# Operands straight from the turned banks, their sums and differences on GpSimd, and the last square from its bank, in a hybrid SSD and attention layer

## The chip, the cores and the metric

The kernel runs on one core of a Trainium2 chip. A core has five engines that work through queues of their own and wait for one another by semaphores: TensorE (PE; its weight loads are listed as PEld), VectorE (DVE), ScalarE (ACT), GpSimd (POOL) and SyncE (SP), which issues most DMAs. Matrix products go to banks of PSUM; VectorE and ScalarE read banks and SBUF tiles, and in this kernel GpSimd reads and writes SBUF tiles only. The metric is the device time of one execution in microseconds, as a median of several runs.

## The reference

One decoder layer of 1024 tokens and 1024 channels, all in float32:

```python
h = _rmsnorm(x, pre_g)
proj = jnp.einsum('bld,de->ble', h, w_in)        # z, xBC, dt, q, k, v, f, gates: 9248 columns
...                                              # branch A: convolution and chunked SSD scan; branch B: attention
merged = jax.nn.sigmoid(g_ssm) * p_ssm + jax.nn.sigmoid(g_att) * p_att
out = jnp.einsum('bld,de->ble', merged, w_out)
return x + _rmsnorm(out, post_g)
```

The change touches the beginning (the norm of x and the operands of the first product) and the very end (the norm of the last 128 rows of the result).

## The kernel before

**Products.** The three large products (w_in, the two branch weights, w_out) are made two output blocks at a time by a seven-product scheme instead of eight products: class `Pair` works on two blocks of 128 output columns (or rows), and its steps 1 to 7 multiply sums of weight blocks with sums of blocks of the other operand. A product keeps float32 accuracy by splitting each operand in a high part (rounded to `fp32r`) and a low part (the rest), and by three matmuls: high by high, low by high, high by low (`matmuls`, with `mm` at line 130). Weights are split by `Pair.split` (lines 351 and 352: ScalarE rounds, VectorE subtracts), sums of weights are made by `total` (line 357). `keep` (line 404) and `give` (lines 412 to 418) take a finished bank out.

**Operands.** For the first product the other operand is the normed x, turned so that channels lie on partitions. With x in four blocks of 512 by 512 (`b11` and `b21` from the first 512 tokens, `b12` and `b22` from the second) the operands are b11, b21, t1 = b12 - b11, -t2 with t2 = b22 - t1, t3 = t2 - b11, t4 = t2 - b21 and -b22. Each has a high tile and a low tile in SBUF with four blocks of 128x512: in the profile x0 is b11, x1 is b21, x2 is -b22, x3 is t1, x4 is -t2, x5 is t3 and x6 is t4, with h or l behind it.

**Prologue** (lines 1132 to 1241). `norm_tiles` squares each 128x1024 tile of x (line 1160 on VectorE for two tiles, line 1162 on ScalarE for the others), makes the reciprocal root (1163, 1164) and scales the tile (1166 on VectorE for the first four tiles, 1168 on GpSimd for the second four). `turned` turns one block of 128 channels of four tiles into a bank `pt` of 128x512 (line 1173; `turn` is line 133), of which there are two. For the first half of the tokens, each of the eight banks is copied into the float32 tile `low`, times pre_norm_g (line 1192 on ScalarE, line 1194 on VectorE for the first two). `put` then makes the high part from `low` (line 1178, ScalarE) and the low part (line 1180, VectorE). For the second half, in four rounds, two banks are copied to `up` and `b22` (line 1212, ScalarE); four float32 matmuls with `wdf` into `df` read `low` and these copies; then come t1 (1218), t2 (1221) and their parts, and the differences t3 and t4, which are written over `low` (1225, 1226, VectorE). Their parts and those of -b22 follow.

**Order.** `Stream` lists all steps of all pairs in one order written out by hand; `halves(n)` issues the next n half steps of six matmuls each. TensorE's queue keeps the order of the program. The queues of the other engines are ordered when the program is built, by the order of the program, by `high_priority` blocks, and by the times that a planner gives to each instruction; `pin` keeps an instruction in the order of the program. On the chip each queue is worked through in that order. In the prologue the stream runs four half steps between the banks 4 to 7 of the first half, one in each of the four rounds, and six after them (the products `pb`, `pd`, `pc`).

**End.** The last four pairs multiply with w_out. For each block of 128 tokens, `outcome` receives two banks of 512 columns as `o[ch]`; `post` squares each (line 1101, ScalarE, with the row's sum in `ssq`), multiplies it by post_norm_g (line 1104) and, after the second one, adds the two sums (1108, VectorE), takes root and reciprocal (1109, 1110), and scales, adds x and stores (1112, 1113). The very last bank is step 4 of the last pair: `give` copies it with its sign turned (line 412, ScalarE) before `post` works on the copy.

Of the kernel before, what the change touches and what calls it, by code (L numbers as in the profile page):

```python
# [16 lines left out]
P = 128  # L17
T = 1024
D = 1024
# [67 lines left out]
def hybrid_layer(ctx: ExitStack, tc, a, out):  # L87
# [50 lines left out]
    def small(name="th"):  # L138
        return gp.tile([P, HALF], F32, tag="th", name=name)
# [182 lines left out]
    class Pair:  # L322
# [7 lines left out]
        def __init__(self, keys, handlers, ops=None, adds=nc.vector):  # L330
            self.keys, self.handlers = keys, handlers
            self.ops = xop if ops is None else ops
            self.adds = adds
            self.raw, self.op, self.prepared = {}, {}, set()
            self.s1, self.sums = None, 0

        def load(self, names):
            for n in names:
# [82 lines left out]
        def do(self, which):  # L421
            if which in (2, 4, 3) or which in (5, 7) and self.sums:
                unit, ch = {2: (0, 0), 4: (1, 0), 3: (0, 1)}.get(which, (1, 1))
                for begin in self.handlers[unit][2:]:
                    begin(ch)
            if which == 1:
                pool, tag = self.bank
                self.b = pool.tile([P, HALF], F32, tag=tag, bufs=1, name="pb")
                yield from self.matmuls(self.b, 1, "b11", True)
                self.k1 = self.keep(self.b)  # L430
            elif which == 2:
                pool, tag = self.other
                ps = pool.tile([P, HALF], F32, tag=tag, bufs=1, name="p" + tag)
                yield from self.matmuls(ps, 2, "b21", True)
                self.give(0, 0, ps, self.k1, "sum")
            elif which == 6:
                yield from self.matmuls(self.b, 6, "-t2", False)
                self.k2 = self.keep(self.b)
            elif which in (5, 7):
                if which == 5:  # L440
                    self.c = pj.tile([P, HALF], F32, tag="c", bufs=1, name="pc")
                    yield from self.matmuls(self.c, 5, "t1", True)
                else:
                    yield from self.matmuls(self.b, 7, "t3", False)
                    self.k7 = self.keep(self.b)
                self.sums += 1
                if self.sums == 2:
                    self.give(1, 1, self.c, self.k7, "less")
            elif which == 4:
                yield from self.matmuls(self.b, 4, "t4", False)  # L450
                self.give(1, 0, self.b)
            elif which == 3:
                yield from self.matmuls(self.c, 3, "-b22", False)
                self.give(0, 1, self.c, self.k2, "from")
# [609 lines left out]
    def merge(i):  # L1064
# [17 lines left out]

        return dst, post, begin

    def outcome(i):

        o, g, xr, st = {}, {}, {}, {}

        def begin(ch):
            xr[ch] = wp.tile([P, KH, P], F32, tag="raw", bufs=6, name="xr").rearrange("p a b -> p (a b)")  # L1090
            nc.sync.dma_start(xr[ch], a["x"][i * P : (i + 1) * P, half(ch)])

        def dst(ch):
            o[ch] = fin["pool"].tile([P, HALF], F32, tag="ot", bufs=5, name="ot")
            return o[ch]

        def post(ch):
# [3 lines left out]
            nc.scalar.activation(small("sq").bitcast(BF16)[:, 0:HALF], o[ch], AF.Square, accum_out=ssq[:, ch : ch + 1])  # L1101

            g[ch] = small("g") if i >= 6 else o[ch]
            (nc.vector if i >= 6 else nc.gpsimd).tensor_tensor(g[ch], o[ch], fin["postg"][:, half(ch)], ALU.mult)
            if len(o) < 2:
                return
            r = ssq[:, 0:1]
            nc.vector.tensor_tensor(r, r, ssq[:, 1:2], ALU.add)
            nc.scalar.activation(r, r, AF.Sqrt, bias=eps4, scale=1.0 / D)
            nc.vector.reciprocal(r, r)  # L1110
            for c in range(2):
                nc.vector.scalar_tensor_tensor(o[c], g[c], r, xr[c], ALU.mult, ALU.add)
                (nc.sync, nc.scalar)[c].dma_start(out[i * P : (i + 1) * P, half(c)], o[c])

        return dst, post, begin

# [7 lines left out]
    def final(kind, i, handler, ops, adds):  # L1124
        return Pair(((kind, 2 * i), (kind, 2 * i + 1)), (handler(2 * i), handler(2 * i + 1)), ops, adds)

    ends = [final("wbs", i, gated, ops_s, nc.vector) for i in range(4)]
    ends += [final("wba", i, merge, ops_a, nc.gpsimd) for i in range(4)]
    ends += [final("merged", i, outcome, ops_w, nc.gpsimd if i > 1 else nc.vector) for i in range(4)]


    with tc.tile_pool(name="pro", bufs=1, reuse_waits="tile", side="right") as pro, tc.tile_pool(
# [23 lines left out]
        def norm_tiles(hf, tiles):  # L1156
            for t, xt in enumerate(tiles, 4 * hf):
                sqt = small("sqt").bitcast(BF16)
                if t in (1, 3):
                    nc.vector.tensor_tensor_reduce(sqt, xt, xt, 1.0, 0.0, ALU.mult, ALU.add, ss[:, t : t + 1])  # L1160
                else:
                    nc.scalar.activation(sqt, xt, AF.Square, accum_out=ss[:, t : t + 1])
                nc.scalar.activation(rstd[:, t : t + 1], ss[:, t : t + 1], AF.Sqrt, bias=epst, scale=1.0 / D)
                nc.vector.reciprocal(rstd[:, t : t + 1], rstd[:, t : t + 1])
                if hf == 0:
                    nc.vector.tensor_scalar(xt, xt, rstd[:, t : t + 1], None, ALU.mult)
                else:
                    nc.gpsimd.tensor_scalar(xt, xt, rstd[:, t : t + 1], None, ALU.mult)

        def turned(tiles, k):  # L1170
            pt = prop.tile([P, HALF], F32, tag="pt", bufs=2, name="pt")
            for j in range(4):
                turn(pt[:, j * P : (j + 1) * P], tiles[j][:, k * P : (k + 1) * P]) 
            return pt
# [13 lines left out]
        stream.begin()  # L1188
        for k in range(NK):
            pt = turned(tiles, k)  # L1190
            if k > 1:
                nc.scalar.activation(low[:, k, :], pt, AF.Copy, scale=preg[:, k : k + 1])
            else:
                nc.vector.tensor_scalar(low[:, k, :], pt, preg[:, k : k + 1], None, ALU.mult)
# [9 lines left out]
        for j in range(KH):  # L1204
# [17 lines left out]
                put("-t2", j, t2, -1.0)  # L1222
            stream.halves(1)

            nc.vector.tensor_tensor(b11, t2, b11, ALU.subtract)
            nc.vector.tensor_tensor(b21, t2, b21, ALU.subtract)
        dft = small("dft")
        nc.scalar.activation(dft, df, AF.Identity, bias=bdf)
        stream.halves(1)
# [470 lines left out]
```

## Time and profile before

| | |
|---|---|
| median of 3 runs | 1325.71 us (1322.34 to 1330.65) |
| profiled execution | 1329.54 us, span 1327.8 us |
| mean granted clock of TensorE | 0.986 |
| busy: TensorE, VectorE, ScalarE, GpSimd | 96%, 77%, 59%, 23% of the span |
| DMA | 233.59 MB, mean 176 GB/s |

The span runs from the first to the last instruction that the profiler recorded. Busy time of TensorE includes waiting inside its pipeline. In rows of the timeline the first number is the start, the second the duration in us, then engine, line, operation, tiles and shapes; in brackets stands the idle time of the engine before it and what ended that. A merged row has "xN" at its end. In rows of groups the numbers after the bar are busy us and mean ns of one. Times are counted from the span's start.

### The profile page before, as it was taken

The page shows a single profiled execution, that of the slowest core. Times are in us where ns is not written, and L with a number is a line of the kernel's source. Part 1 is how long each engine was busy: PE and PEld are TensorE (multiplying, and loading weights), DVE is VectorE, ACT ScalarE, POOL GpSimd, SP SyncE. Part 2 cuts the span into 40 slices and gives each one's busy share as a digit, 9 for nine tenths or more (in the row PEclk, how much of TensorE's full clock was granted, in tenths as well). Part 3 has the DMA queues.
Part 4 walks back from the last instruction along what each step waited for, and adds up shares of the span by engine and source line. Part 5 has one row for each costly group of instructions (what it writes and reads, how often), then busy time and mean ns, then how long its engine had stood idle before and what let it go on. Part 6 is the DMA issues. An engine that isn't in the chain of part 4 may idle for free.

```text
span 1327.8 us, 21035 instructions
## 1 busy us (share of the span) xinstructions
PE 1271.5 (96%) x7054; PEld 995.1 (75%) x7054; DVE 1021.1 (77%) x1977; ACT 789.8 (59%) x1726; POOL 304.2 (23%) x311
## 2 busy tenths in 40 slices
PE   6899999999999999899999999999989998899997
PEld 4578888788878788688777677777766776678886
DVE  6878888798789878787767667666788666886975
ACT  7645665566556756566555565666666555644654
POOL 3000340024102410142001223131111212246152
PEclk9899999999999999899999999999999999999999
DMA  8132543645363546345464557565677556656933
GB/s 289 59 115 67 161 141 120 195 136 150 127 206 128 136 148 186 115 124 184 164 231 159 196 172 236 200 206 180 225 244 240 194 181 230 223 176 200 364 125 103
DMA packets 154668, 233.59 MB, mean 176 GB/s; under 512 B 17216, under 2 KB 62656, under 8 KB 154560
## 3 DMA queue, kind: packets, MB, share of 16 engines
q1 hardware_dynamic: 142016, 205.53, 48.4%
q0 software_dynamic: 6400, 16.10, 3.2%
q10 hardware_dynamic: 6144, 10.62, 2.1%
q8 instruction: 55, 0.90, 0.3%
q14 instruction: 53, 0.43, 0.1%
HBM read 162.99 MB, written 72.34 MB: 177 GB/s over the span
## 4 chain that ended last, share of the span: by engine, by line
PE 64%; DVE 11%; DMA 10%; ACT 8%; issue 5%; SPq 1%; POOL 0%; DVEq 0%; ACTq 0%
PE pb L130 26%; PE pc L130 14%; PE pd L130 5%; PE av L130 4%; PE s L130 4%; PE pt L133 4%; ACT ex L1463 2%; PE yps L130 2%; DMA raw<-in_wu 2%; DVE wop L352 2%; ACT wop L351 1%; DVE sum L357 1%; PE tr L133 1%; PE st L130 1%; DVE ex L1459 1%
## 5 line engine op out<-in xcount | busy, mean ns | idle before, releaser
L1463 ACT ACTIVATE ex<-ex,nm 128x512 f32<-128x512 f32 (+1 forms) x192 | 116.1, 607 | 146.7 <-DVE nm L1459 142.7
L352 DVE TENSOR_TENSOR wop<-sum,wop 128x512 fp32r<-128x512 f32 x178 | 141.4, 795 | 66.0 <-ACT wop L351 65.4
L351 ACT ACTIVATE wop<-sum 128x512 fp32r<-128x512 f32 x178 | 111.4, 626 | 77.7 <-DVE sum L357 25.6
L404 ACT ACTIVATE s<-pb 128x512 f32<-128x512 f32 x144 | 85.2, 592 | 93.7 <-PE pb L130 89.9
L352 DVE TENSOR_TENSOR wop<-raw,wop 128x512 fp32r<-128x512 f32 x146 | 107.0, 734 | 42.7 <-ACT wop L351 41.6
L130 PE MATMUL pc<-x3h,wop 128*128 128x512 f32 x384 | 131.8, 401 | 1.9 <-DVE th L418 0.9
L130 PE MATMUL pb<-x0h,wop 128*128 128x512 f32 x384 | 133.0, 404 | 0.0
L130 PE MATMUL pb<-x6h,wop 128*128 128x512 f32 x384 | 131.2, 399 | 1.2 <-ACT s L404 1.2
L130 PE MATMUL pb<-x4h,wop 128*128 128x512 f32 x384 | 130.2, 396 | 0.7 <-ACT x4h L1178 0.7
L130 PE MATMUL pc<-x2h,wop 128*128 128x512 f32 x384 | 130.4, 398 | 0.3 <-DVE u L756 0.3
L130 PE MATMUL pb<-x5h,wop 128*128 128x512 f32 x384 | 129.1, 395 | 0.7 <-ACT s L404 0.7
L1459 DVE CUSTOM_DVE_ANT_0 ex<-s,fb 128x512 f32<-128x512 f32 (+1 forms) x192 | 95.7, 552 | 33.1 <-PE s L130 33.1
L351 ACT ACTIVATE wop<-raw 128x512 fp32r<-128x512 f32 x146 | 90.7, 623 | 12.7 <-PE pc L130 6.4
L133 PE MATMUL pt<-ident,ex 128*128 128x128 f32 x576 | 80.5, 285 | 11.6 <-ACT ex L1463 10.6
L130 PE MATMUL pd<-x1h,wop 128*128 128x512 f32 x272 | 91.2, 394 | 0.0
L130 PEld LDWEIGHTS pc<-x3h,wop 128*128 128x128 f32 x384 | 73.3, 191 | 20.5 <-ACT wop L351 1.9
L133 PEld LDWEIGHTS pt<-ident,ex 128*128 128x128 f32 x576 | 68.9, 145 | 24.8 <-ACT ex L1463 19.2
L130 PEld LDWEIGHTS pb<-x6h,wop 128*128 128x128 f32 x384 | 73.0, 190 | 18.3 <-ACT s L404 1.6
L130 PEld LDWEIGHTS pb<-x0h,wop 128*128 128x128 f32 x384 | 74.3, 193 | 16.5 <-issue 0.7
L130 PEld LDWEIGHTS pb<-x4h,wop 128*128 128x128 f32 x384 | 72.3, 188 | 17.5 <-ACT x4h L1178 1.2
L213 POOL TENSOR_TENSOR wd<-wd 128x256 f32<-128x256 f32 x32 | 32.7, 1021 | 229.7 <-DMA wd<-in_wo 128.9
L130 PEld LDWEIGHTS pb<-x5h,wop 128*128 128x128 f32 x384 | 72.1, 188 | 17.4 <-ACT s L404 1.1
(310 smaller groups left out, 3021.2 us busy)
## 6 DMA issues: line engine op xcount, KB each, us to landing
raw<-in_wu SPq DMA_DIRECT2D x128, 256.0 KB, 3.5
csb<-cs_dram SPq DMA_DIRECT2D x32, 256.0 KB, 5.1
fb<-f_dram SPq DMA_DIRECT2D x16, 512.0 KB, 6.7
rb<-st_dram SPq DMA_DIRECT2D x48, 128.0 KB, 3.0
wd<-in_wo SPq DMA_DIRECT2D x40, 128.0 KB, 3.3
xt<-in_x SPq DMA_DIRECT2D x8, 512.0 KB, 5.9
gs_dram<-th ACTq DMA_DIRECT2D x16, 256.0 KB, 4.0
qh_dram<-th SPq DMA_DIRECT2D x16, 256.0 KB, 4.8
```

The source lines that it names most:

```text
L130: return tc.keep_in_program_order(nc.tensor.matmul(*args, **kw))
L133: return tc.keep_in_program_order(nc.tensor.transpose(out_, in_, idn))
L213: pin(nc.gpsimd.tensor_tensor(t[out_], t[a_], t[b_], ALU.subtract))
L351: nc.scalar.activation(op[:, 0], src, AF.Copy)
L352: nc.vector.tensor_tensor(op[:, 1], src, op[:, 0], ALU.subtract)
L357: self.adds.tensor_tensor(t, x, y, ALU.add)
L404: nc.scalar.activation(s, ps, AF.Copy)
L1459: nc.vector.tensor_tensor_reduce(o, s[e][:, 0:w], fb[hp, h][:, e, 0:w], 1.0, 3.0e38, ALU.add, ALU.min, nm)
L1463: pin(nc.scalar.activation(o, o, AF.Exp, scale=-1.0, bias=nm, accum_out=hd.at(hd.sm, i, h, e)))
```

## The change

Four edits in the prologue and one at the end:

- The four tiles of the second half are scaled by VectorE too, no longer by GpSimd.
- For the first half, ScalarE makes the high part from the bank itself (times pre_norm_g), VectorE makes the low part from the bank and the high part, and GpSimd then adds the two into `low`. The copy into `low` and the use of `put` on it go. A bank is free only once the low part is made; there are three banks `pt` instead of two.
- The differences t3 and t4 are made by GpSimd instead of VectorE.
- Of the last block of 128 tokens (i = 7), the last bank is no longer copied: ScalarE squares it where it is, VectorE multiplies it by -1 and post_norm_g, and the sum of squares of the other half enters the root as its bias, scaled beforehand.

```diff
@@ class Pair, step 4
-                self.give(1, 0, self.b)
+                (self.closing or (lambda ps: self.give(1, 0, ps)))(self.b)
@@ outcome
+        def finish(r):
+            nc.vector.reciprocal(r, r)
+            for c in range(2):
+                nc.vector.scalar_tensor_tensor(o[c], g[c], r, xr[c], ALU.mult, ALU.add)
+                (nc.sync, nc.scalar)[c].dma_start(out[i * P : (i + 1) * P, half(c)], o[c])
+
+        def closing(ps):
+
+            r, g[0] = st["ssq"][:, 0:1], small("g")
+            with tc.high_priority():
+                nc.scalar.activation(dst(0).bitcast(BF16)[:, 0:HALF], ps, AF.Square, accum_out=r)
+                nc.vector.scalar_tensor_tensor(g[0], ps, -1.0, fin["postg"][:, half(0)], ALU.mult, ALU.mult)
+                nc.scalar.activation(r, r, AF.Sqrt, bias=st["ssq"][:, 1:2], scale=1.0 / D)
+                finish(r)
...
+            if i == 7:
+                nc.vector.tensor_scalar(ssq[:, ch : ch + 1], ssq[:, ch : ch + 1], 1.0 / D, eps4, ALU.mult, ALU.add)
...
+    ends[-1].closing = closings[7]
@@ prologue
-                if hf == 0:
-                    nc.vector.tensor_scalar(xt, xt, rstd[:, t : t + 1], None, ALU.mult)
-                else:
-                    nc.gpsimd.tensor_scalar(xt, xt, rstd[:, t : t + 1], None, ALU.mult)
+                nc.vector.tensor_scalar(xt, xt, rstd[:, t : t + 1], None, ALU.mult)
...
-            pt = prop.tile([P, HALF], F32, tag="pt", bufs=2, name="pt")
+            pt = prop.tile([P, HALF], F32, tag="pt", bufs=3, name="pt")
...
-            if k > 1:
-                nc.scalar.activation(low[:, k, :], pt, AF.Copy, scale=preg[:, k : k + 1])
-            else:
-                nc.vector.tensor_scalar(low[:, k, :], pt, preg[:, k : k + 1], None, ALU.mult)
-            put("b11" if k < KH else "b21", k % KH, low[:, k, :])
+            h, l = (p[:, k % KH, :] for p in xop["b11" if k < KH else "b21"])
+            nc.scalar.activation(h, pt, AF.Copy, scale=preg[:, k : k + 1])
+            nc.vector.scalar_tensor_tensor(l, pt, preg[:, k : k + 1], h, ALU.mult, ALU.subtract)
+            nc.gpsimd.tensor_tensor(low[:, k, :], h.bitcast(F32), l.bitcast(F32), ALU.add)
...
-            nc.vector.tensor_tensor(b11, t2, b11, ALU.subtract)
-            nc.vector.tensor_tensor(b21, t2, b21, ALU.subtract)
+            nc.gpsimd.tensor_tensor(b11, t2, b11, ALU.subtract)
+            nc.gpsimd.tensor_tensor(b21, t2, b21, ALU.subtract)
```

More of the change, by code (lines that the diff above doesn't have):

```diff
@@ L334, in __init__ @@
             self.raw, self.op, self.prepared = {}, {}, set()
-            self.s1, self.sums = None, 0
+            self.s1, self.sums, self.closing = None, 0, None
         def load(self, names):
@@ L1083, in merge @@
         return dst, post, begin
+    closings = {}
     def outcome(i):
@@ L1095, in dst @@
             return o[ch]
+        def finish(r):
[10 more added lines that the diff above has]
+                finish(r)
+        closings[i] = closing
         def post(ch):
@@ L1109, in post @@
             nc.scalar.activation(r, r, AF.Sqrt, bias=eps4, scale=1.0 / D)
[L1110 to L1113, printed above, removed]
+            finish(r)
         return dst, post, begin
```

## The prediction, made before the change was run

> **What bounds the kernel now.** I read the page first, then the busy times of the stages around the edits, then the chain that ended last, then the timeline where two engines meet.
>
> ```profile
> PE 1271.5 (96%) x7054; PEld 995.1 (75%) x7054; DVE 1021.1 (77%) x1977; ACT 789.8 (59%) x1726; POOL 304.2 (23%) x311
> ```
> TensorE sets the time almost everywhere. An edit without TensorE work can only move the places where TensorE stands or runs slowly, and both edited places are such: the prologue and the last microseconds. The table by stretch (after the length: PE, PEld, DVE, ACT, POOL, granted clock, DMA share, GB/s):
>
> ```profile
> 12.00:30.00 18.00, 15.51 (x65) 11.75 (x67) 14.45 (x23) 17.30 (x35) 12.24 (x4) 1.00 0.86 314
> 30.00:46.50 16.50, 16.50 (x79) 8.75 (x78) 14.90 (x24) 10.96 (x17) 0.00 (x0) 1.00 0.09 34
> 46.50:60.60 14.10, 11.06 (x37) 8.22 (x35) 13.39 (x22) 10.14 (x19) 0.00 (x0) 0.76 0.23 79
> ```
> In the first stretch, which turns the first half of x, ScalarE is busy 17.30 of 18.00 us. In the second, with the other half, TensorE is full. In the third VectorE is full (13.39 of 14.10) and TensorE has 11.06, at a clock of 0.76. The chain of waits agrees (start, us, what):
>
> ```profile
> 16.99 0.58 ACT low L1192
> 17.62 1.12 PE pt L133 x4
> ...
> 44.93 1.59 PE pd L130 x6
> ...
> 49.04 0.60 DVE low L1225
> 49.64 0.60 DVE low L1226
> ...
> 51.45 0.60 DVE x4l L1182
> ...
> 60.02 0.60 DVE wop L352
> ```
> From 46.5 to 60.6 us VectorE's queue is the chain; two of its pieces are differences that the change moves. What TensorE does meanwhile:
>
> ```profile
> 49.31 0.50 PE L130 MATMUL pb<-x4h,wop 128*128 128x512 f32 x1 [0.75 <-ACT x4h L1178]
> 52.10 0.79 PE L130 MATMUL pb<-x4l,wop 128*128 128x512 f32 x1 [2.29 <-DVE x4l L1182]
> ```
> It stands for 0.75 + 2.29 = 3.0 us until the low part of -t2 is there. The clock lost in that stretch is (1 - 0.76) x 14.1 = 3.4 us. So 6.4 us of TensorE's time hang on VectorE there.
>
> **The change part by part.** I cost it against the span of 1327.8 us, in a profiled execution of 1329.54 us; that lies 3.8 us over the median of 1325.71, so the difference is then put on the median. The groups of 12 to 60.6 us that are edited:
>
> ```profile
> L1192 ACT ACTIVATE low<-pt,preg 128x512 f32<-128x512 f32 x6 | 4.0, 681 | 0.0
> L1178 ACT ACTIVATE x0h<-low 128x512 fp32r<-128x512 f32 x4 | 2.4, 623 | 0.0
> L1194 DVE TENSOR_SCALAR low<-pt,preg 128x512 f32<-128x512 f32 x2 | 1.5, 750 | 0.6 <-PE pt L133 0.6
> L1225 DVE TENSOR_TENSOR low<-th,low 128x512 f32<-128x512 f32 x4 | 2.7, 685 | 0.0
> L1226 DVE TENSOR_TENSOR low<-th,low 128x512 f32<-128x512 f32 x4 | 2.7, 684 | 0.0
> L1166 DVE TENSOR_SCALAR xt<-xt,rstd 128x1024 f32<-128x1024 f32 x1 | 0.8, 754 | 0.0
> L1168 POOL TENSOR_SCALAR xt<-xt,rstd 128x1024 f32<-128x1024 f32 x4 | 12.2, 3065 | 13.6 <-DVE rstd L1164 13.6
> ```
> ScalarE: six copies into low go (4.1 us); eight high parts now read the bank with a scale, 681 instead of 623 ns by the nearest rows, +0.5. Net -3.6 us of its 17.30.
>
> VectorE, own work: two copies into low go (-1.5), eight differences go (-5.4), four scalings of x come (4 x 0.75 = +3.0). The eight low parts read the bank instead of low. No row has this very form; I take it at no change, between 0.69 (a subtraction that reads a bank, L416, quoted below) and 0.75 (L1194), at most +0.5 in all.
>
> GpSimd: four scalings go (-12.2), eight sums and eight differences of 128x512 come, 16 x 1.30 = 20.8 us by the row of 1296.36 below. None of them issues a DMA, and GpSimd has nothing else to do there: its next instruction is
>
> ```profile
> 60.84 0.29 POOL L1252 TENSOR_SCALAR_AFFINE_SELECT tri<-onesr 128x128 f32<-128x128 f32 x1 [33.62 <-DVE u L756]
> ```
> So by engine totals the change looks good: the two full engines lose 3.6 and 3.9 us. What decides is what happens when GpSimd and VectorE run side by side:
>
> ```profile
> 1296.36 1.30 POOL L357 TENSOR_TENSOR sum<-sum,merged 128x512 f32<-128x512 f32 x1 [2.55 <-DVE wop L352]
> 1297.13 0.69 DVE L416 TENSOR_TENSOR ot<-pc,s 128x512 f32<-128x512 f32 x1 [0.92 <-ACT s L404]
> ...
> 1303.44 1.29 POOL L1104 TENSOR_TENSOR ot<-ot,postg 128x512 f32<-128x512 f32 x1
> 1304.17 1.11 DVE L352 TENSOR_TENSOR wop<-sum,wop 128x512 fp32r<-128x512 f32 x1 [0.68 <-ACT wop L351]
> ...
> 1306.77 1.64 POOL L1104 TENSOR_TENSOR ot<-ot,postg 128x512 f32<-128x512 f32 x1 [2.04 <-ACT sq L1101]
> 1307.18 1.78 DVE L352 TENSOR_TENSOR wop<-merged,wop 128x512 fp32r<-128x512 f32 x1
> ```
> L352 reads two tiles of SBUF. Begun while GpSimd is in a two-input operation, it takes 1.11 or 1.78 us, and ends 0.5 us after GpSimd's. L416 reads one bank and one tile: 0.69 us in the same situation. So a two-input operation on GpSimd stops VectorE's two-tile operations until it is done, at a price of up to 1.78 - 0.69 = 1.09 us. Leaving the difference on VectorE costs 0.68 us; giving it to GpSimd costs VectorE between 0 and 1.09 us. The old scalings on GpSimd were milder:
>
> ```profile
> 14.19 8.50 POOL L1168 TENSOR_SCALAR xt<-xt,rstd 128x1024 f32<-128x1024 f32 x3 [12.83 <-DVE rstd L1164]
> ...
> 15.28 0.69 DVE L1180 TENSOR_TENSOR x0l<-low,x0h 128x512 fp32r<-128x512 f32 x1 [0.40 <-ACT x0h L1178]
> ...
> 17.30 1.39 DVE L357 TENSOR_TENSOR sum<-raw 128x512 f32<-128x512 f32 x1 [0.63 <-DMA raw<-in_wu]
> ...
> 19.92 2.20 DVE L1180 TENSOR_TENSOR x0l<-low,x0h 128x512 fp32r<-128x512 f32 x2 [0.36 <-ACT x0h L1178]
> ```
> Against 0.69 each (1.29 for a merged pair that overlaps by 0.09) they cost 0.70 + 0.91 = 1.6 us, which the change gives back. The Trainium skill, "SBUF — State Buffer", section "Who interferes with whom", says that the one that issues first has the shared pair for the whole instruction. The trace agrees for two-input operations, but not for the scaling: L1180 at 15.28 runs undisturbed 1.1 us into a 2.8 us scaling. By the page the price of a wait is the full 1.30 us, and the 16 waits could come to 20.8 us instead of 17.4.
>
> *First stretch.* VectorE: 14.45 - 1.5 - 1.6 + 3.0 = 14.35 us, plus eight sums at 0 to 1.09 us each. About half of what VectorE does there (weight halves, sums of weights) reads two tiles, while the low parts now read one tile and the bank; I take half the price, 4.4 us: 18.7 us in 18.0. So the saving on ScalarE is not cashed, since VectorE is now as full as ScalarE was: +0.7 us. Bounds: with no waits TensorE's 15.51 us become the limit, -2.5; with all of them 23.1 us of VectorE, 8.6 more than before. The third bank lets the fifth transposition start before 17.62, but what follows needs the low parts from VectorE.
>
> *Second and third stretch.* VectorE has 14.90 + 13.39 = 28.3 of 30.6 us. Less 5.4, plus 8 x 1.09 = 8.7: here nearly every operation (t1, t2, the low parts, weight halves, sums) reads two tiles, so I take the full price. That is 31.6 us: 1.0 over if all idle time is filled, 3.3 if the 2.3 us stay as they are; I take +2.2. What is late next is the low part of -t2 (x4l) and the parts of t3, whose high parts ScalarE can only start when GpSimd has done the difference; behind them in ScalarE's queue stand bank copies and weight halves for TensorE. Bounds: no waits, and TensorE gets its 6.4 us back; all of them, and +3.3 us, with a second stretch of slow clock (3.4 us again) if a new gap opens.
>
> *The end.*
>
> ```profile
> 1320.98 0.60 ACT L412 ACTIVATE ot<-pb 128x512 f32<-128x512 f32 x1 [0.69 <-PE pb L130]
> 1321.61 0.63 ACT L1101 ACTIVATE sq<-ot 128x512 bf16<-128x512 f32 x1
> ...
> 1322.14 0.19 ACT L1101 ACTIVATION_READ_ACCUMULATOR sq<-ot 128x1 f32 x1
> 1322.45 0.15 DVE L1108 TENSOR_TENSOR ssq<-ssq 128x1 f32<-128x1 f32 x1
> 1322.64 0.29 ACT L1109 ACTIVATE ssq<-ssq,eps 128x1 f32<-128x1 f32 x1 [0.31 <-DVE ssq L1108]
> ```
> The copy goes, so the square starts at 1320.98 instead of 1321.61: -0.63 us. The addition of the two sums goes (the other half enters as the root's bias), so the root follows the accumulator at 1322.33 - 0.63 instead of 1322.64: -0.31 us. The product with postg runs on VectorE beside the square. Together -0.9 us, all on the path, give or take 0.2.
>
> Sum: +0.7 + 2.2 - 0.9 = +2.0 us, 1331.5 for the profiled execution, 1327.7 us on the median.
>
> **The rivals.** *Faster: the waits find cover.* If VectorE stands idle, or reads a bank, when GpSimd works, the waits cost nothing and the freed time counts: at most -2.5, -6.4 and -0.9, which is -9.8 us, or 1315.9. With half of the first two, -5.4 us, 1320.3. For it speaks that VectorE's own work falls in both places; against it that it was 90% busy there with two-tile operations.
>
> *Much slower: the waits add up in a fixed order.* Each engine works through a queue whose order is fixed when the program is built. If the t3 parts stand ahead of x4l, VectorE waits for ScalarE, that one for GpSimd, and TensorE for x4l. All 16 waits with no idle filled give 8.6 + 3.3 = +11.9 us; a second stretch at a low clock adds 3.4; less 0.9 it is +14.4, or 1340.1. It decides once nearly every sum meets a two-tile operation. Against it: the sums follow low parts whose successors read the bank.
>
> *No effect but the end.* If VectorE's gains and waits cancel, -0.9: 1324.8.
>
> *The new order is not used.* If the squares of the second half stay ahead of the high parts on ScalarE, these come no earlier, and the first stretch gains nothing; my sum holds without that gain.
>
> **How the numbers follow.** Forecast 0.45, faster 0.25, much slower 0.2, end only 0.1. The range is 1316 to 1341 us: the far ends of the two rivals with the runs' scatter, which was 1322.34 to 1330.65 before. The forecast by itself is good for 1322 to 1333. About 1% (13 us) is what a measurement of this kernel can tell from no change. Faster by more than that needs the rival's far end and a lucky run, 0.06; slower by more needs most of the second rival and a tail of the forecast, 0.18; within it 0.76.
>
> **What would show it.** Right: 16 two-input operations on GpSimd of 1.3 to 1.8 us between 14 and 50 us; among VectorE's two-tile operations there eight or more of 1.1 to 1.8 us; VectorE over 90% busy from 30 to 61 us; TensorE still standing before a product with x4l, with the clock below 1 after it; the final root starting 0.9 us sooner after the last matmul. Wrong: VectorE's operations at 0.69 throughout, TensorE without a gap near 50 us, or the first product pb before 16 us with TensorE's second half starting 2 us sooner.

## The result, and the profile after

The changed kernel takes 1335.82 us (1335.43 to 1340.78, six runs), the kernel before beside it 1325.01 us (1322.34 to 1330.65): a ratio of 1.0086, 95% interval 1.0059 to 1.0113. In a second set of runs it was 1337.39 against 1328.67 us, 1.0068 (1.0047 to 1.0088). So the change costs 9 to 11 us. The forecast was +2.0: the direction and the range hold, the size does not. The median also lies outside the 1322 to 1333 us for which the forecast by itself was good, and nearer to the slower rival (1340.1) than to the forecast (1327.7). The profiled execution took 1340.78 us, the longest of the six; its span is 1339.1.

The first part of the page of the changed kernel, busy time by engine:

```profile
PE 1273.3 (95%) x7054; PEld 993.6 (74%) x7054; DVE 1032.0 (77%) x1971; ACT 785.3 (59%) x1719; POOL 322.1 (24%) x323
```
TensorE does the same 7054 matmuls, in the same order; VectorE is busy 10.9 us longer with six instructions fewer. The windows of the prologue in the changed kernel (columns as in the prediction):

```profile
12.00:30.00 18.00, 13.80 (x62) 10.78 (x62) 16.64 (x23) 14.01 (x28) 10.07 (x7) 1.00 0.84 302
30.00:46.50 16.50, 14.00 (x59) 6.40 (x59) 16.20 (x19) 9.42 (x15) 10.60 (x7) 1.00 0.14 50
46.50:60.60 14.10, 12.77 (x59) 9.02 (x57) 13.55 (x18) 11.98 (x23) 5.74 (x4) 1.00 0.16 56
60.60:83.30 22.70, 17.84 (x68) 14.87 (x69) 20.15 (x48) 6.88 (x14) 1.03 (x2) 0.77 0.29 96
```
ScalarE is relieved as intended (17.30 to 14.01 in the first row), and the full engine is now VectorE: 16.64, 16.20 and 13.55 us. The clock of 0.76 at 46.5 to 60.6 us is gone (1.00), and it comes back one row later (0.77). That stretch in the kernel before, from its windows:

```profile
60.60:83.30 22.70, 22.07 (x100) 17.79 (x99) 19.65 (x51) 11.35 (x21) 0.54 (x2) 1.00 0.31 105
```
So the loss sits at the seam between the prologue and what follows. TensorE there in the changed kernel, from the timeline:

```profile
58.88 0.39 PE L130 MATMUL pb<-x5h,wop 128*128 128x512 f32 x1
65.46 1.94 PE L130 MATMUL pt_df<-summing,dft 128*128 128x64 f32 x8 [6.19 <-DVE u L756]
67.16 0.77 PE L130 MATMUL pc<-x2h,wop 128*128 128x512 f32 x1
67.74 0.63 PE L130 MATMUL pc<-x2l,wop 128*128 128x512 f32 x1
```
And in the kernel before, the same instructions:

```profile
60.48 0.39 PE L130 MATMUL pb<-x5h,wop 128*128 128x512 f32 x1
60.90 1.10 PE L130 MATMUL pt_df<-summing,dft 128*128 128x64 f32 x8
...
62.62 0.39 PE L130 MATMUL pc<-x2l,wop 128*128 128x512 f32 x1
```
The last matmul ahead of `pt_df` comes 1.6 us *earlier* than before (58.88 against 60.48): the stand of 3.0 us before x4l is gone, as moving the differences promised. But x4l itself starts no sooner (51.76 against 51.36 us): TensorE comes into this stretch 4.6 us late, its first pb<-x4h at 50.95 instead of 46.34, and so made up 6.2 us by 58.88. With the differences left on VectorE (below, e1) TensorE is as late there, x4l comes at 55.78, and the stand is back. After 58.88 TensorE stands for 6.19 us before `pt_df`, which needs `summing`, two halves of an identity that VectorE adds at the end of its queue. `pt_df` starts 4.56 us late, and the matmuls behind it take 0.63 us instead of 0.39. The chain of waits of the changed kernel shows what VectorE did meanwhile (start, us, what):

```profile
57.80 2.48 DVE x2l L1198 x4
...
61.41 1.88 DVE x6l L1196 x3
...
65.10 0.14 DVE onesr L1264
65.24 0.08 DVE summing L1280
...
65.46 1.94 PE pt_df L130 x8
```
Its queue is one unbroken chain up to `summing`. The memset of `onesr` just ahead of that stands at 60.60 in the kernel before and at 65.07 here; it serves below as the mark of how late VectorE is. Where the time went in that queue, from VectorE's timeline in the changed kernel:

```profile
14.81 1.80 DVE L1184 TENSOR_SCALAR xt<-xt,rstd 128x1024 f32<-128x1024 f32 x1
...
19.10 1.77 DVE L357 TENSOR_TENSOR sum<-raw 128x512 f32<-128x512 f32 x1
...
27.36 0.74 DVE L1184 TENSOR_SCALAR xt<-xt,rstd 128x1024 f32<-128x1024 f32 x1
...
31.99 1.77 DVE L1233 TENSOR_TENSOR th<-up,low 128x512 f32<-128x512 f32 x1
...
52.48 1.78 DVE L352 TENSOR_TENSOR wop<-sum,wop 128x512 fp32r<-128x512 f32 x1
```
The scaling at 27.36 is undisturbed; the other rows are among the longest of 16 operations that took clearly longer than undisturbed ones of their kind (0.68 us; 0.75 for a scaling). The groups of GpSimd's new work between 12 and 60.6 us (busy us, mean ns):

```profile
L1210 POOL TENSOR_TENSOR low<-x0h,x0l 128x512 f32<-128x512 f32 x4 | 5.9, 1487 | 16.0 <-DVE rstd L1183 13.4 <-DVE x0l L1209 2.6
...
L1241 POOL TENSOR_TENSOR low<-th,low 128x512 f32<-128x512 f32 x4 | 6.9, 1726 | 0.0
```
They too are longer than the 1.30 us of the prediction's row. Summed over VectorE's timeline, the excess is 5.8 us beside the sums and 6.5 beside the differences: 12.3 in all.

At the other end, VectorE's last rows in the changed kernel, whose last matmul starts at 1332.29:

```profile
1332.26 1.41 DVE L1102 SCALAR_TENSOR_TENSOR ot<-g,ssq,xr 128x512 f32<-128x512 f32 x2
1333.59 0.68 DVE L1110 SCALAR_TENSOR_TENSOR g<-pb,postg 128x512 f32<-128x512 f32 x1
1334.19 0.15 DVE L1100 RECIPROCAL ssq<-ssq 128x1 f32<-128x1 f32 x1
1334.38 1.42 DVE L1102 SCALAR_TENSOR_TENSOR ot<-g,ssq,xr 128x512 f32<-128x512 f32 x2
```
ScalarE's root in the changed kernel, and the last scalings in the kernel before, whose last matmul starts at 1320.55:

```profile
1333.44 0.29 ACT L1111 ACTIVATE ssq<-ssq 128x1 f32<-128x1 f32 x1
```
```profile
1323.16 1.42 DVE L1112 SCALAR_TENSOR_TENSOR ot<-g,ssq,xr 128x512 f32<-128x512 f32 x2
```
From the last matmul the root comes 1.15 us later instead of 2.09 (its row of 1322.64 is in the prediction): the promised 0.94. But the scalings come 2.09 instead of 2.61 us after it, 0.52 sooner. The product g and the reciprocal stand in VectorE's queue behind the scalings of the block before (1332.26, 1.41 us).

### The profile page after: what moved, and what is told of

Same layout as the page of the kernel before. It is cut to its first block, busy times and chain, and to the rows that moved or that the text cites. A ratio compares the mean times of both kernels' runs of the same rounds, so it can differ in the third digit from the quotient of the medians.

```text
span 1339.1 us, 21038 instructions
## 1 busy us (share of the span) xinstructions
PE 1273.3 (95%) x7054; PEld 993.6 (74%) x7054; DVE 1032.0 (77%) x1971; ACT 785.3 (59%) x1719; POOL 322.1 (24%) x323
## 4 chain that ended last, share of the span: by engine, by line
PE 61%; DVE 12%; DMA 11%; issue 8%; ACT 7%; SPq 1%; POOL 0%; DVEq 0%; ACTq 0%
PE pb L130 25%; PE pc L130 14%; PE pd L130 5%; PE av L130 4%; PE s L130 3%; PE pt L133 3%; ACT ex L1478 2%; DVE wop L352 2%; PE yps L130 2%; DMA raw<-in_wu 2%; ACT wop L351 1%; DMA st_dram<-st 1%; PE tr L133 1%; DVE sum L357 1%; DVE ex L1474 1%
## 5 line engine op out<-in xcount | busy, mean ns | idle before, releaser
L352 DVE TENSOR_TENSOR wop<-sum,wop 128x512 fp32r<-128x512 f32 x178 | 147.1, 827 | 66.0 <-ACT wop L351 65.6
L404 ACT ACTIVATE s<-pb 128x512 f32<-128x512 f32 x144 | 85.1, 591 | 93.2 <-PE pb L130 88.6
L130 PEld LDWEIGHTS pb<-x5h,wop 128*128 128x128 f32 x384 | 72.5, 189 | 18.3 <-ACT s L404 1.7
L130 PEld LDWEIGHTS pc<-x2h,wop 128*128 128x128 f32 x384 | 73.2, 191 | 17.2 <-issue 0.9
```

Source lines behind the costliest of these rows:

```text
L130: return tc.keep_in_program_order(nc.tensor.matmul(*args, **kw))
L352: nc.vector.tensor_tensor(op[:, 1], src, op[:, 0], ALU.subtract)
L404: nc.scalar.activation(s, ps, AF.Copy)
```

## The experiments

Two theories. **A: VectorE is late** because its operations beside GpSimd's two-input operations wait, and the constant at the end of its queue hands the delay to TensorE. **B: something else is late**, either operands that now come out of GpSimd or ScalarE's queue, whose order the build changed. This table holds all twelve runs, the columns being the median, the ratio to the kernel before on the same chip, what that ratio makes of 1328 us, and from the profiles the start of VectorE's memset of onesr and of TensorE's first product pb<-x6h, shortly behind the seam. Executions of one kernel differ by up to 7.5 us from their median, so ratios go by medians of 6 to 12 runs (about 30 of the kernel before); the two starts come from one execution each. (The first profile of the changed kernel has 65.07 and 72.4.)

| kernel | median us (runs) | ratio, 95% interval | us | onesr | x6h |
|---|---|---|---|---|---|
| before | 1328.2 (31) | 1 | 0 | 60.60 | 65.1 |
| changed, again (after_again) | 1337.39 (6) | 1.0068, 1.0047 to 1.0088 | +9.0 | 65.25 | 71.7 |
| before + unread subtractions (e5) | 1333.92 (10) | 1.0045, 1.0028 to 1.0062 | +6.0 | 65.67 | 70.1 |
| changed, differences on VectorE (e1) | 1332.29 (12) | 1.0029, 1.0013 to 1.0045 | +3.9 | 65.01 | 69.6 |
| changed, low by ScalarE (e2) | 1332.33 (9) | 1.0035, 1.0016 to 1.0054 | +4.6 | 64.02 | 71.0 |
| changed, both: no GpSimd (e4) | 1329.12 (12) | 1.0007, 0.9987 to 1.0026 | +0.9 | 62.51 | 66.9 |
| before + scaling on VectorE (e8) | 1330.86 (12) | 1.0011, 0.9993 to 1.0029 | +1.5 | 62.08 | 66.1 |
| before + parts from the bank (e9) | 1332.36 (12) | 1.0024, 1.0004 to 1.0044 | +3.2 | 65.25 | 69.9 |
| before + the end (e3) | 1327.64 (12) | 0.9996, 0.9975 to 1.0016 | -0.5 | 59.98 | 64.0 |
| changed, pt_df freed (e6) | 1329.70 (12) | 1.0015, 0.9998 to 1.0032 | +2.0 | 65.00 | 68.9 |
| changed, tanh later (e10) | 1334.07 (10) | 1.0046, 1.0028 to 1.0064 | +6.1 | 64.76 | 71.3 |
| changed, both of these (e11) | 1332.44 (12) | 1.0026, 1.0011 to 1.0040 | +3.5 | 64.69 | 67.6 |
| before + the end, pt_df freed (e12) | 1323.61 (12) | 0.9966, 0.9951 to 0.9981 | -4.5 | 60.87 | 65.5 |

**Contention by itself.** The kernel before, with eight subtractions on GpSimd that nobody reads, two per round:

```diff
+            for m in range(2):
+                nc.gpsimd.tensor_tensor(scratch, xop["-t2"][0][:, j, :].bitcast(F32), xop["b11"][m][:, j, :].bitcast(F32), ALU.subtract)
             nc.vector.tensor_tensor(b11, t2, b11, ALU.subtract)
             nc.vector.tensor_tensor(b21, t2, b21, ALU.subtract)
```


> The kernel before, with eight more subtractions on GpSimd, two at the end of each of the four rounds between 30 and 60 us, into a spare tile that nobody reads; VectorE keeps its own differences, and the queues of TensorE, ScalarE, VectorE and SyncE are as before. The theory that VectorE's operations beside a two-input operation of GpSimd wait for it: eight waits of 0.7 to 1.09 us, 5.6 to 8.7 in all, of which the some 3 us that VectorE idles before 60 us take a part; its memset of onesr, at 60.60 in the kernel before, comes 3 to 6 us later, TensorE stands that long before the first pt_df, and the time rises by 3 to 6 us (1332 to 1335). The theory that what comes late in the changed kernel is what waits for GpSimd's results, or the order of ScalarE's queue: nobody waits for these, so the memset stays within 0.5 us of 60.60 and the time within 1 us.

VectorE's timeline in this kernel:

```profile
32.54 1.77 DVE L1231 TENSOR_TENSOR low<-th,low 128x512 f32<-128x512 f32 x1
34.24 1.76 DVE L1183 SCALAR_TENSOR_TENSOR x4l<-th,x4h 128x512 fp32r<-128x512 f32 x1
...
39.11 1.16 DVE L1231 TENSOR_TENSOR low<-th,low 128x512 f32<-128x512 f32 x1
40.20 1.76 DVE L1183 SCALAR_TENSOR_TENSOR x4l<-th,x4h 128x512 fp32r<-128x512 f32 x1
...
48.50 1.18 DVE L1181 TENSOR_TENSOR x3l<-th,x3h 128x512 fp32r<-128x512 f32 x1
49.60 1.76 DVE L352 TENSOR_TENSOR wop<-sum,wop 128x512 fp32r<-128x512 f32 x1
51.29 1.75 DVE L1181 TENSOR_TENSOR x5l<-low,x5h 128x512 fp32r<-128x512 f32 x1
52.96 1.74 DVE L1230 TENSOR_TENSOR low<-th,low 128x512 f32<-128x512 f32 x1
```
Eight subtractions, eight waits of 0.5 to 1.1 us, 7.4 us in all; the memset 5.07 us later, the time 6.0 us longer. Nobody depends on these results, and no queue but GpSimd's has another instruction or another order, so B cannot explain it: A's mechanism exists, at 0.93 us a wait, where the prediction took at most 1.09. The expected place of the loss was wrong, though: TensorE loses the 5 us at a product with the low part x4l and then finds `summing` in time. Its row in this kernel, 52.10 in the kernel before:

```profile
57.16 0.80 PE L130 MATMUL pb<-x4l,wop 128*128 128x512 f32 x1 [6.20 <-DVE x4l L1183]
```

**GpSimd's two jobs taken back.** The changed kernel with the differences on VectorE, with `low` copied from the bank by ScalarE instead of the sums, and with both:

```diff
-            nc.gpsimd.tensor_tensor(b11, t2, b11, ALU.subtract)
-            nc.gpsimd.tensor_tensor(b21, t2, b21, ALU.subtract)
+            nc.vector.tensor_tensor(b11, t2, b11, ALU.subtract)
+            nc.vector.tensor_tensor(b21, t2, b21, ALU.subtract)
```
```diff
-            nc.gpsimd.tensor_tensor(low[:, k, :], h.bitcast(F32), l.bitcast(F32), ALU.add)
+            nc.scalar.activation(low[:, k, :], pt, AF.Copy, scale=preg[:, k : k + 1])
```


> The changed kernel (1335.8 us), with the eight differences t3 and t4 back on VectorE. Theory A (GpSimd's two-input operations stop VectorE): in the changed kernel the waits beside the differences add up to 6.4 us of VectorE's time, doing them itself costs it 8 x 0.6 = 4.8 us; so VectorE's last prologue operation (the memset of onesr, 65.07 us) comes about 1.6 us sooner and the time falls by 1 to 2 us, to about 1334. Theory B (the results come late, because GpSimd needs 1.3 us and not 0.6): those who wait for t3 and t4 would gain, 3 us or more. Theory C (another order of the queues is what costs): no bound, but the order of the other operations then differs.

> The changed kernel, with low copied from the bank by ScalarE (as before the change) in place of GpSimd's eight sums; high and low parts still come from the bank, the differences stay on GpSimd. Theory A: the waits beside the sums add up to 5.8 us of VectorE's time and go, ScalarE has 4 us idle before 30 us for 8 x 0.58 us of copies; VectorE's memset of onesr comes 4 to 6 us sooner, the time falls to 1329 to 1332 us. Theory B: low is there sooner by under 1 us, the time falls by under 1 us. If a bank is held longer by the copy, the first products come later by up to 1 us.

> The changed kernel with both kinds of operation off GpSimd: low copied by ScalarE, differences on VectorE; the parts from the bank, the scaling by VectorE, the third bank and the end stay. Theory A: 12.2 us of waits go and 4.8 us of work come back, so VectorE's memset of onesr moves from 65.1 to about 58 us, where TensorE becomes the limit; the time is 1321 to 1325 us, at or below the kernel before. Theory B: 1331 to 1334 us. Theory C (the order, or something after the prologue): stays above 1330 us.

Each alone takes the loss from 9.0 to 4 or 5 us, both to +0.9, which is no difference that can be told. The two halves are not additive. The expectations by theory A's count of VectorE's time were missed: the memset was to come near 63.5, at 59 to 61 and at 58 us and came at 65.01, 64.02 and 62.51, and the kernel with both was to take 1321 to 1325 us and took 1329.12. Nor do these three runs separate the theories, because ScalarE's order differs among them: in e4 the copy b stands ahead of the first table load, as in the kernel before; in e1, e2 and the changed kernel it stands behind (below, "ScalarE's order"). ScalarE in e4:

```profile
41.12 0.68 ACT L1227 ACTIVATE b<-pt,preg 128x512 f32<-128x512 f32 x1
41.82 1.28 ACT L620 ACT_TABLE_LOAD   x1
```
Two things are learnt beside that. Without either job of GpSimd nothing is gained over the kernel before (e4), so the parts from the bank, in this form, show no profit even without contention. And the first kernel's memset is as late (65.01) as the changed one's, though its VectorE isn't full (busy 43.58 of the 48.6 us from 12 to 60.6, with 42.74 in the kernel before), while its time is 0.4% shorter. TensorE in it:

```profile
53.73 0.51 PE L130 MATMUL pb<-x4h,wop 128*128 128x512 f32 x1 [0.77 <-ACT x4h L1194]
56.52 0.79 PE L130 MATMUL pb<-x4l,wop 128*128 128x512 f32 x1 [2.29 <-DVE x4l L1198]
...
65.40 1.08 PE L130 MATMUL pt_df<-summing,dft 128*128 128x64 f32 x8
```
With the differences back ahead of x4l the old stand of 3.0 us returns, TensorE reaches `pt_df` without a stand, at the same 65.4 us, and `pt_df` takes 1.08 instead of 1.94. x6h starts at 69.6 instead of 72.4. So at an equal delay of VectorE the one long stand costs 2 to 3 us more than the two short ones, by the slow clock behind it: with the differences back the slow clock (0.50 from 55.2 to 62.1 us, then 1.00) is over before `pt_df`, for which TensorE would have had to wait anyway.

**The seam.** The changed kernel with `pt_df` made by two accumulating products with the halves of the identity, so that it needs nothing from VectorE:

```diff
-            mm(pt[:, c * 64 : (c + 1) * 64], dft[:, c * P : (c + 1) * P], summing, start=True, stop=True)
+            for n in range(2):
+                mm(pt[:, c * 64 : (c + 1) * 64], dft[:, c * P : (c + 1) * P], ident[:, 64 * n : 64 * n + 64], start=n == 0, stop=n == 1)
...
-        nc.vector.tensor_tensor(summing, ident[:, 0:64], ident[:, 64:P], ALU.add)
```


> The changed kernel, with the product pt_df freed from VectorE: its right operand (the sum of two halves of ident, made at the end of VectorE's prologue queue) is replaced by two accumulating products with the halves themselves. Theory A with the clock (VectorE's queue is what everyone waits for; the 6.2 us gap stood before pt_df only because that operand is last in the queue, and the slow clock after it, 2.7 us, came on top): TensorE starts pt_df near 59.5 us, waits in smaller pieces, the clock stays up, and the time falls by 3 to 5 us. If the length of VectorE's queue alone counts, whatever TensorE does before: under 1.5 us.

TensorE in it:

```profile
59.04 1.89 PE L130 MATMUL pt_df<-ident,dft 128*128 128x64 f32 x16
64.48 0.80 PE L130 MATMUL pc<-x2h,wop 128*128 128x512 f32 x1 [3.55 <-DVE th L416]
```
VectorE is as late as ever (65.00), but TensorE does `pt_df` meanwhile, and then stands 3.55 us for the next thing that VectorE has late (`th`, L416). The ratio falls from 1.0068 to 1.0015, 7 us where 3 to 5 were expected, of which x6h shows 2.8; where the rest comes from is not shown. With the tanh moved, freeing `pt_df` takes the ratio only from 1.0046 to 1.0026 (below; these intervals overlap). So part of the loss passes through this one dependency, which is theory A's second half; how large a part is not settled.

**The other edits alone.** The scaling of the second half on VectorE, the parts straight from three banks with `low` by ScalarE, and the end, each added to the kernel before:

```diff
-                    nc.gpsimd.tensor_scalar(xt, xt, rstd[:, t : t + 1], None, ALU.mult)
+                    nc.vector.tensor_scalar(xt, xt, rstd[:, t : t + 1], None, ALU.mult)
```


> The kernel before, with the scaling of the second four tiles of x by VectorE alone. By the ledger VectorE gets 3.0 us of work and loses 1.6 us of waits in the first stretch: +1.4 us on VectorE, at most +1.5 us in time; the memset of onesr at 60.6 to 62 us.

```diff
-            pt = prop.tile([P, HALF], F32, tag="pt", bufs=2, name="pt")
+            pt = prop.tile([P, HALF], F32, tag="pt", bufs=3, name="pt")
...
+            nc.scalar.activation(h, pt, AF.Copy, scale=preg[:, k : k + 1])
+            nc.vector.scalar_tensor_tensor(l, pt, preg[:, k : k + 1], h, ALU.mult, ALU.subtract)
+            nc.scalar.activation(low[:, k, :], pt, AF.Copy, scale=preg[:, k : k + 1])
```


> The kernel before, with high and low parts straight from the banks and three banks, low copied by ScalarE for all eight; scaling and differences as before the change, no sums. ScalarE has two more copies (+1.2 us), VectorE two fewer (-1.3 us); the third bank and the shorter chain could let the first products start before 18.4 us. ScalarE was the limit up to 30 us, so +0 to +1.5 us in time.

```diff
+                (self.closing or (lambda ps: self.give(1, 0, ps)))(self.b)
...
+            if i == 7:
+                nc.vector.tensor_scalar(ssq[:, ch : ch + 1], ssq[:, ch : ch + 1], 1.0 / D, eps4, ALU.mult, ALU.add)
```


> The kernel before, with the edit of the end alone. The prediction counted -0.9 us; the trace of the changed kernel shows 0.5 us from the last matmul to the last scaling, because the product with postg and the reciprocal stand behind the two scalings of the block before in VectorE's queue. So -0.5 us, within the scatter; the last matmul ends as before.

The scaling and the end cannot be told from nothing; the parts alone cost 3.2 us (0.5 to 5.8), more than the 0 to 1.5 expected. None of these edits shows a gain by itself; the sums and the differences on GpSimd were not added to the kernel before alone. The parts alone also show a late memset without a full VectorE: it comes at 65.25, 4.65 us late, with VectorE busy 37.06 of the 48.6 us from 12 to 60.6. No operation was added on GpSimd there, but the table load stands ahead of b as in the changed kernel, and TensorE waits:

```profile
44.11 1.04 PE L130 MATMUL df<-b,wdf 128*32 128x512 f32 x2 [1.47 <-ACT b L1211]
```

> The changed kernel once more, timed beside the ones below. Its profile had TensorE 7.3 us behind the kernel before at 72 us, 0.5 us gained at the end, and 4.4 us more lost in between, where the queues of the two kernels hold the same order; the eight-differences kernel lost 3.1 us less than nothing there. If that part is scatter between executions, the median lies 6 to 8 us over before (ratio 1.005 to 1.006) and this profile's drift after 72 us differs from 4.4 us; if something of the change lives on there, ratio 1.0085 again and again 4 us.

This repetition confirms the loss and shows the scatter between profiles: the span is 1333.0 instead of 1339.1 us, although the stand before `pt_df` is 6.20 us again. The ratio lies between the two expected, and its interval holds both; the drift of 4.4 us after 72 us did not come again.

**ScalarE's order.** In the kernel before, ScalarE's timeline reads:

```profile
38.73 0.68 ACT L1212 ACTIVATE b<-pt,preg 128x512 f32<-128x512 f32 x1
39.42 1.28 ACT L620 ACT_TABLE_LOAD   x1
40.72 0.63 ACT L620 ACTIVATE th<-th 128x512 f32<-128x512 f32 x1
```
and in the changed kernel:

```profile
41.50 1.28 ACT L620 ACT_TABLE_LOAD   x1
42.80 0.63 ACT L620 ACTIVATE th<-th 128x512 f32<-128x512 f32 x1
43.33 0.67 ACT L1227 ACTIVATE b<-pt,preg 128x512 f32<-128x512 f32 x1
```
The build placed the table load and the first tanh ahead of the copy b, for which TensorE's df<-b of the third round waits. That was theory B's best case: df<-b starts 4.6 us late there, of which the two rows that went ahead make 1.9. TensorE in the kernel before and in the changed one:

```profile
39.46 1.04 PE L130 MATMUL df<-b,wdf 128*32 128x512 f32 x2
```
```profile
44.06 1.04 PE L130 MATMUL df<-b,wdf 128*32 128x512 f32 x2 [1.47 <-ACT b L1227]
```
The changed kernel was run with the tanh issued later, alone and with `pt_df` freed:

```diff
+            if dram is gs_dram and i == 0 and ch == 0:
+                stream.after(3, lambda: squash(ch, pin))
...
+                if k >= KH:
+                    pin(copy)
```


> The changed kernel, with the first tanh and its table load moved behind the copies b of the third and the fourth round in ScalarE's queue; all else but three neighbours in VectorE's queue is as in the changed kernel. The theory that ScalarE's queue order costs: the matmuls df of the third round come 1.9 us earlier (the 1.28 of the table load and 0.63 of the tanh), VectorE's memset of onesr by as much, and the time falls by 2 to 3 us (1334 to 1335 where the changed kernel has 1337). The theory that VectorE's queue alone sets the end of the prologue, because it is full from 30 to 65 us: df comes 1.9 us earlier, the memset stays within 0.5 us of 65.1, the stand before pt_df grows from 6.2 to about 8 us, and the time stays within 1 us of the changed kernel's.

> The changed kernel with both: the first tanh behind the copies b, and pt_df as two accumulating products with the halves of the identity, without the operand from VectorE. Were VectorE's queue the only limit, it comes out as the version with pt_df freed alone: ratio 1.0015 to the kernel before, about 1329.7 to 1330. If ScalarE's order costs TensorE 1.9 us that nothing takes back once pt_df is free, the ratio is 0.9995 to 1.0005, about 1328 to 1329.

TensorE in the version with the tanh alone moved:

```profile
42.40 1.04 PE L130 MATMUL df<-b,wdf 128*32 128x512 f32 x2
...
65.15 1.94 PE L130 MATMUL pt_df<-summing,dft 128*128 128x64 f32 x8 [4.73 <-DVE summing L1288]
```
df<-b comes 1.66 us earlier, but the memset only 0.31 (64.76) and `pt_df` 0.31: VectorE's queue, which is full, decides. The stand did not grow to 8 us as expected; it shrank to 4.73, since TensorE stands 1.00 us a little earlier for a copy of ScalarE (L404). The memset is where the second theory had it; the time, 2.9 us shorter, is what the first expected, but the intervals overlap (1.0046 against 1.0068), and with `pt_df` freed the moved tanh is not better (1.0026 against 1.0015). So the order costs 1.7 us at its place, and what it costs at the end is not settled.

The order also bears on the runs above. The load stands ahead of b in the changed kernel, e1, e2, e6, e8 and e9, and behind it in the kernel before, e3, e4, e5, e10, e11 and e12. Among those with it behind, the changed kernel with the tanh later (e10, +6.1 us, VectorE full) and the one without GpSimd's two jobs (e4, +0.9) have intervals apart from each other: 1.0028 to 1.0064 against 0.9987 to 1.0026. Together with the unread subtractions (e5, +6.0) this is what shows that GpSimd's operations cost 5 to 6 us without the moved load. What the moved load adds in e1 and e9, where VectorE waits instead of being full, no run separates.

**A version that beats both.** The kernel before with the end of the changed one and with `pt_df` freed (both diffs stand above):

> The kernel before with the end of the changed one (the last tile's square from its bank) and pt_df freed from VectorE; nothing of the prologue's other edits. If the end of VectorE's queue already holds TensorE in the kernel before, the stand of about 1 us at 60.3 goes, and the slow clock at 60.6 to 62 with it: 1 to 2 us faster than the kernel before (1326.5 to 1327.5), of which 0.5 is the end's. If it held nothing there, the time is that of the end alone, 0.5 us faster or the same (ratio 0.9996).

It takes 1323.61 us, ratio 0.9966 (0.9951 to 0.9981): faster than both kernels, and by more than either expectation gave. TensorE at the seam in it:

```profile
60.99 1.89 PE L130 MATMUL pt_df<-ident,dft 128*128 128x64 f32 x16
```
That is where the kernel before has it (60.90), so the profile does not show the gain at the seam; x6h even starts at 65.5. Against the profile of before, the difference builds up in steps between 390 and 1110 us, where both kernels have the same instructions. The two largest lie where the kernel before ran at a lower clock in its profiled execution: 0.66 against 0.83 from 550 to 560 us, 0.83 against 1.00 from 740 to 750. Such steps come without any edit ahead of them too ("The sum" below), so one pair of profiles can't explain the medians. The end gives 0.5 us; where the other 4 come from stays open.

## Why the prediction was right, and where it was not

**What bounds the kernel: right, with one error.** The prologue and the end are where the time moved. But the 6.4 us that "hang on VectorE" at 46.5 to 60.6 us were counted, in the bounds and in the faster rival, as if TensorE could have them. They went (the stand before x4l is gone, the clock there is 1.00, and 6.2 us were made up), and TensorE was 1.6 us ahead at 58.88; then it waited for the end of the very same queue, at the memset of onesr. The row of 60.84 us in the prediction already named a constant made by VectorE; the step did not ask what TensorE needs next from VectorE after x4l. Those 6.4 us were cover: nothing could be gained from them with VectorE's queue as long as it was.

**GpSimd's waits: right, the sum partly by luck.** 13.1 us were taken for 16 operations (4.4 and 8.7); 12.3 were measured (5.8 and 6.5), and eight idle subtractions alone made 7.4. The first half was taken too low and the second too high, and the errors cancel. The bound of 1.09 us for one wait held (longest 1.10). By the whole-instruction rule of the Trainium skill, "SBUF — State Buffer", section "Who interferes with whom", the wait could reach GpSimd's full 1.3 to 1.7 us; these runs show at most 1.1. Even the scaling at 14.81, which starts 0.02 us after a GpSimd operation of 1.27 us, took only 1.05 us more than an undisturbed one. That the scaling of x would wait too was not foreseen (1.80, 1.14 and 1.06 us instead of 0.75), and it makes 1.75 of the 5.8.

**VectorE's idle time: mis-sized.** Own work and waits make +8.1 us of busy time up to the memset: 16.64 + 16.20 + 13.55 + 4.47 = 50.86 against 14.45 + 14.90 + 13.39 = 42.74. The prediction's own terms give +7.6. It let idle time absorb all but 2.9 of that (0.7 and 2.2); in fact 5.86 us of idle became 2.21, so 3.65 were absorbed and 4.47 were left. That is 1.6 us of the error.

**The clock after a new stand: the term that failed.** It stood in the bounds ("a second stretch of slow clock (3.4 us again) if a new gap opens") and not in the sum. The gap opened: 6.19 us, and TensorE went from 4.56 us late at `pt_df` to 7.3 at x6h, so 2.7 us; in the second profile, from 4.74 to 6.5, so 1.8. In the kernel with the differences back, equally late on VectorE but without the long stand, nothing is lost there: from `pt_df` to x6h it takes 4.2 us, as the kernel before does.

**The end: mis-sized.** The root came 0.94 us sooner, as worked out; VectorE's fixed order (g and the reciprocal behind the scalings of the block before) kept 0.4 of it. "On VectorE beside the square" was the step that failed; alone the end measures -0.5 us, with an interval that holds 0.

**The sum.** 4.56 + 2.7 - 0.5 = +6.8 us are accounted for by rows, in the second profile 4.74 + 1.8 - 0.5 = +6.0, against +2.0 predicted and +9 to +11 measured. The remaining 3 to 4 us have no place: in one profile TensorE drifts a further 4 us behind after 72 us, in the other profile of the changed kernel it does not. Such drift needs no edit of the prologue: in the kernel with the end alone x6h starts 1.1 us ahead of the kernel before and the last matmul, at 1325.04, is 4.5 behind. Whether the 3 to 4 us are scatter or belong to the change is not shown. In ten of the eleven other kernels of the table (all but the last), the delay of x6h against before agrees with the time to within 2 us.

**The rivals.** The likeliest of the rest was "the waits add up in a fixed order" (+14.4). Its place was off, since x4l was not what came late, but its mechanism is what happened: a fixed queue on VectorE, a new stand, a slow clock. The measured time lies between it and the forecast, nearer to it; that the direction came out right is owed to the waits, that the range held to its width. The faster rival fell with its premise that VectorE would find idle time. ScalarE's order was raised only for the squares; what moved was the table load.

**The signs named.** Right: sixteen operations on GpSimd of 1.3 to 1.8 us (one took 2.32), more than eight long ones on VectorE, VectorE over 90% busy from 30 to 61 us, the root 0.94 us sooner. Wrong: TensorE does not stand before x4l, and the clock there is 1.00; it stands before `pt_df`. "TensorE without a gap near 50 us" was on the prediction's own list of signs against it, and came true.

## What to carry to other kernels

Before giving an elementwise operation to an idle GpSimd, cost it at what the neighbouring engine loses: here 16 operations that took 6.9 us of work from VectorE (8 differences and 2 copies) put 12.3 us of waits on it. When a stand on the critical engine is removed, follow the late engine's queue to the next thing it owes; a constant of 0.15 us at its end can take everything back. Freeing that constant cost 0.8 us of TensorE (1.89 instead of 1.10 for `pt_df`). The kernel before with `pt_df` freed, and the new end, is the fastest one measured, but that the freeing makes it so is not shown. And where a build orders the queues by planned times, compare the other queues' orders too before putting a difference down to the edit.

## What the runs showed of the hardware

The slow clock can set in before a stand of TensorE is over, and it does not last equally long behind equal stands. In the changed kernel the granted clock is 0.99 from 59.3 to 62.3 us, 0.50 from 62.3 to 72.5 and 1.00 after that: 7.1 us of it lie behind the stand of 6.19 us, where the matmuls took 0.63 instead of 0.39 us. In its second profile, with a stand of 6.20 us, it is 1.00 to 63.7 and 0.50 to 70.5: 4.9 us lie behind. This fits the 2.7 and 1.8 us lost there. In the kernel with `pt_df` freed, 3.55 us were followed by 3.4 us at 0.50. The kernel before and the one with the end alone have the same stands near 50 us (0.75 and 0.77, then 2.29 each) and a clock of 0.76 and 0.88 from 46.5 to 60.6 us.

VectorE's one-input scaling of 128x1024 waits beside GpSimd's two-input operations as two-tile operations do: 1.80 against 0.74 us. And GpSimd is slowed as well: its operations averaged 1.49 to 1.87 us in the prologue, against 1.30 in the prediction's row of 1296.36.
